# A batched matrix-product trace on one core: program layout, one-turn loops, and a third of the copies on VectorE

## The chip, the core and the metric

The kernel runs on one core of a Trainium2 chip. The core has TensorE (PE, a 128x128 matrix unit that writes to PSUM), VectorE (DVE), ScalarE (ACT), GpSimd (POOL, which here issues nearly all transfers) and SyncE (SP), each with its own stream of instructions; they meet through semaphores. Sixteen DMA engines move data between HBM and the on-chip SBUF; a transfer is spread over them in packets. The metric is the device time of one execution in microseconds (us).

## The reference

```python
B, N = 8, 2176
def reference(a, b):                       # a, b: (8, 2176, 2176) float32
    prod = np.matmul(a, b)
    traces = np.diagonal(prod, axis1=1, axis2=2).sum(axis=-1)
    return traces.astype(np.float32)       # (8,)
```

Only the trace is wanted, so no product is formed: for each batch the result is the sum over i and k of a[i, k] * b[k, i], that is, the elementwise product of a transposed with b, summed. All of a and b has to be read once, 303 MB in float32.

## The kernel before

The matrices are read with a cast to bf16 on the way (POOL issues, L182). 2176 is 17 blocks of 128. The rows of a matrix are taken in three groups of 6, 6 and 5 blocks (`six` for the two of 6, `five` for the last). For each of the eight batches:

- POOL loads the five-block part of a into `rows_b` (`five`) and the twelve-block part into `a_six`; then, as soon as the parts are free again, the five-block and the twelve-block part of b, both into `rows_b`. The waits ahead of these issues (on `made`, the count of finished transposes, and on `product`, the count of finished products) are what lets a buffer be written again.
- TensorE transposes a in 26 tiles (L226 to L246), 8 from `five` and 18 from `a_six`, into three PSUM slots (`SLOTS = 3`, tile n uses slot n % 3). Pairs of bf16 columns are moved as one float32 (L242), the odd ones as bf16 (L245). [...]
- ScalarE (L276) and VectorE (L302) copy the slots to `at`, the transposed a. VectorE takes the tiles with n % 4 == 3, ScalarE the other 20. The semaphores `free[k]` give the slot back to TensorE.
- VectorE multiplies `at` with b and sums (L291), once for the five-block part and once for the twelve-block part.

The last batch is closed differently: its b comes in ten pieces (`pieces`, semaphores `d_late`), from five blocks down to a part of one. VectorE takes the first 13 blocks' worth of columns of each row block, TensorE the other four by matrix products accumulated into `trace_ps`, whose diagonal holds what is wanted (L250 to L262: one product with zeros that opens the sum, a loop of 16 turns at L252 that waits on `landed`, and twelve products for the last row block). VectorE then takes the diagonal (L291 with `identity32`), TensorE adds over partitions (L332), VectorE reduces to eight numbers (L334) and SP stores them (L339).

In the order of the program, TensorE has the large loop first, then the products that close the last batch, then the total. The programs of ScalarE, VectorE and POOL are unrolled over the eight batches without a loop. POOL's ends with 20 increments of a semaphore `unread` that no one waits for, and a drain, after which the region ends for all engines.

Of the kernel before, what the change touches and what calls it, by code (L numbers as in the profile page):

```python
# [22 lines left out]
def kernel(  # L23
# [6 lines left out]
    nc = tc.nc  # L30
    P = 128
    BATCH, N, N2 = a.shape
# [84 lines left out]
    def rows_of(src, start, m, r0, r1):  # L117
        return src[start:start + P * m, :].rearrange("(p r) k -> p (r k)", r=m)[:, r0 * N:r1 * N]
# [25 lines left out]
    with tc.tile_critical(no_gpsimd_drain=True):  # L144
        def counted(name):
            return Counted(nc, name)

        unread = nc.alloc_semaphore("unread")
# [32 lines left out]
        def fetch(count, dst, src):  # L181
            count.by(gp.dma_start(out=dst, in_=src), 16)  # L182

        for n in range(BATCH):
            if n == 0:
                fetch(d_a5, flat(five[:, 1:, :]), rows_of(a[0], TWICE * P, FIVE, 1, FIVE))
                fetch(d_a6, a_six.rearrange(by_twos, g=2), six(a[0]))
                tc.wait_critical_data_deps()
                gp.wait_ge(zeros.sem, 2)
                for t in (identity32, identity16):  # L190
                    ready.by(gp.affine_select(
                        out=t, in_=t, compare_op=mybir.AluOpType.not_equal, fill=1.0, base=0,
                        pattern=[[-1, P]], channel_multiplier=1,
                    ))
            else:
                gp.wait_ge(product.sem, 2 * n - 1)
                fetch(d_a5, flat(five), rows_of(a[n], TWICE * P, FIVE, 0, FIVE))
                gp.wait_ge(made, EACH * n)
                if n < LAST:
                    fetch(d_a6, a_six.rearrange(by_twos, g=2), six(a[n]))  # L200
                else:
# [5 lines left out]
            gp.wait_ge(made, EACH * n + HEAD)  # L207
            if n < LAST:
                fetch(d_b5, flat(five), rows_of(b[n], TWICE * P, FIVE, 0, FIVE))
                if n:  # L210
                    gp.wait_ge(product.sem, 2 * n)
                fetch(d_b6, b_six.rearrange(by_twos, g=2), six(b[n]))
                continue
            for k, piece in enumerate(pieces):
                if k == 1:
                    gp.wait_ge(product.sem, 2 * n)
                fetch(d_late[k], piece.dst, piece.src)
        for _ in range(20):
            gp.sem_inc(unread)
        gp.drain()  # L220


        pe = nc.tensor
        pe.wait_ge(ready.sem, 3)
        alone = OrderedEngineSet([pe.engine])
        with nc.Fori(0, BATCH, engines=alone, hint_back_edge=True):  # L226
            for n, (moves, _, _) in enumerate(tiles):
                use, k = divmod(n, SLOTS)
                ps = slots[k]
                if n == 0:  # L230
                    pe.wait_ge(moved, 1)
                if use:
                    pe.wait_ge(free[k], 1 + use)
                else:
                    pe.wait_ge(free[k], 1 + uses[k]).then_inc(free[k], -uses[k])  # L235
                if n == HEAD:
                    pe.wait_ge(moved, 2)
                elif n == NECK:
                    pe.wait_ge(moved, 3).then_inc(moved, -3)
                for dtype, place, src in moves:  # L240
                    if dtype == f32:
                        last = pe.transpose(ps[:, place, :], src, identity32)  # L242
                    else:
                        ps16 = ps.bitcast(bf16).rearrange("q a b -> q (a b)")
                        last = pe.transpose(ps16[:, place * P:(place + 1) * P], src, identity16)  # L245
                last.then_inc(made, 1)  # L246

        pe.wait_ge(scalar_done.sem, BATCH)
        pe.wait_ge(vector_done.sem, BATCH)
        pe.matmul(trace_ps, diagonal, diagonal, start=True, stop=False)  # L250
        x, y = flat(at), flat(rows_b)
        with nc.Fori(SHARE, SHARE + END * N, N, engines=alone, hint_back_edge=True) as first:  # L252
            pe.wait_ge(landed, 1).then_inc(landed, -1)  # L253
            for c in range(ON_TENSOR):
                block = bass.ds(first + c * P, P)
                pe.matmul(trace_ps, x[:, block], y[:, block], start=False, stop=False)  # L256
        for k, piece in enumerate(pieces):
            if piece.v1 == NT:
                pe.wait_ge(d_late[k].sem, 16)
                for c in range(N - CLOSE * P if piece.hi == N else piece.lo, piece.hi, P):  # L260
                    block = slice(END * N + c, END * N + c + P)
                    ins = pe.matmul(  # L262
                        trace_ps, x[:, block], y[:, block],
                        start=False, stop=piece.lo == 0 and c + P == piece.hi,
                    )
        added.by(ins)


        act = nc.scalar
        for n in range(BATCH):  # L270
            for t in on_scalar:
                _, dst, view = tiles[t]
                if t == on_scalar[0] and n:
                    act.wait_ge(product.sem, 2 * n)
                act.wait_ge(made, EACH * n + t + 1)
                ins = act.copy(out=dst, in_=view(slots[t % SLOTS]))  # L276
                if t != on_scalar[-1]:
                    ins.then_inc(free[t % SLOTS], 1)
                else:
                    scalar_done.by(ins)  # L280


        dve = nc.vector
# [9 lines left out]
                op0=MUL, op1=ADD, accum_out=acc,  # L293
            )

        for n in range(BATCH):
            for t in on_vector:
                _, dst, view = tiles[t]
                if t == on_vector[0] and n:
                    dve.wait_ge(product.sem, 2 * n)  # L300
                dve.wait_ge(made, EACH * n + t + 1)
                ins = dve.tensor_copy(out=dst, in_=view(slots[t % SLOTS]))  # L302
                if t != on_vector[-1]:
                    ins.then_inc(free[t % SLOTS], 1)
                else:
                    vector_done.by(ins)
            dve.wait_ge(vector_done.sem, n + 1).then_inc(free[on_vector[-1] % SLOTS], 1)
            dve.wait_ge(scalar_done.sem, n + 1).then_inc(free[on_scalar[-1] % SLOTS], 1)  # L308
            if n == LAST:
                continue  # L310
            for k, (load, t, v0) in enumerate(((d_b5, five, 0), (d_b6, b_six, FIVE))):
                dve.wait_ge(load.sem, 16 * (n + 1))
                product.by(multiply_reduce(
                    flat(at[:, v0:v0 + t.shape[1], :]), flat(t), sums[:, TAKEN * n + k:TAKEN * n + k + 1],
                ))
        taken = TAKEN * LAST
        for k, piece in enumerate(pieces[:len(whole) + 1]):
            if piece is whole[-1]:
                dve.wait_ge(parts.sem, k)
                parts.by(dve.reduce_sum(  # L320
                    out=sums[:, taken:taken + 1], in_=late[:, 0:k], axis=mybir.AxisListType.X,
                ))
            close = piece.v1 == NT
            acc = sums[:, taken + 1 + close:taken + 2 + close] if close or piece is whole[-1] else late[:, k:k + 1]
            dve.wait_ge(d_late[k].sem, 16)
            x, y = (t[:, piece.v0:piece.v1, piece.lo:N - CLOSE * P if close else SHARE] for t in (at, rows_b))
            parts.by(multiply_reduce(x, y, acc))
        dve.wait_ge(added.sem, 1)
        parts.by(multiply_reduce(identity32, trace_ps, sums[:, taken + 3:], out=diagonal))

        pe.wait_ge(parts.sem, parts.count)
        summed.by(pe.matmul(total, ones, sums, start=True, stop=True))  # L332
        dve.wait_ge(summed.sem, 1)
        resulted.by(dve.reduce_sum(  # L334
            out=result[:1, :], in_=total.rearrange("o (b n) -> o b n", n=TAKEN),
            axis=mybir.AxisListType.X,
        ))
        sp.wait_ge(resulted.sem, 1)
        stored.by(sp.dma_start(  # L339
            out=out.rearrange("(a b) -> a b", a=1), in_=result[:1, :],  # L340
# [36 lines left out]
```

## Time and profile before

| | us |
|---|---|
| median of three runs (707.38 to 708.32) | 707.7 |
| profiled execution | 707.8 |
| its span, first to last instruction of the program | 705.8 |
| PE busy | 207.5 |
| DVE busy | 382.5 |
| ACT busy | 205.9 |
| POOL busy | 25.5 |

The span is shorter than the profiled execution's time by 2.0 us, which lie outside the program's own instructions. The busy times of the compute engines are shares of a span in which the transfers run all the time; the view by queue gives 152.12 MB written to SBUF (the half of what is read, by the cast) at a mean of 216 GB/s. In that view a queue is a row with its number of packets, the megabytes and the time of its packets as a share of 16 engines; the kind "instruction" is the transfer of program code to an engine's sequencer, "software_dynamic" are POOL's loads, "hardware_dynamic" the few that ACT and SP issue. Cut to a window, the same view counts the packets that start in it. In rows of the timeline the columns are start, duration, engine, line and operation, shapes, count, and in brackets the idle time before with what ended it; in the chain of waits they are start, duration and what the chain passed through.

### The profile page before, as it was taken

The numbers are of one execution on the slowest core, as the hardware profiler recorded it, in microseconds if no ns is written. First come the engines' busy times: TensorE is split into PE (matmuls) and PEld (weight loads), VectorE is DVE, ScalarE is ACT, GpSimd is POOL, SyncE is SP. The second block draws the span as 40 slices with busy tenths as digits, with TensorE's granted clock in tenths as the row PEclk, the third lists the DMA queues.
The fourth block names the chain that finished last, engine by engine and source line by source line (L and its number), as shares of the span: only waits on it lengthen the run. The fifth ranks groups of instructions, "written<-read, shape, count | busy, mean of one in ns | idle before, by whom it ended". The sixth has DMA issues, their size and how long they took to land.

```text
span 705.8 us, 3821 instructions
## 1 busy us (share of the span) xinstructions
PE 207.5 (29%) x1575; PEld 184.1 (26%) x1575; DVE 382.5 (54%) x101; ACT 205.9 (29%) x162; POOL 25.5 (4%) x47
## 2 busy tenths in 40 slices
PE   0335013440134401244013430124301353015633
PEld 0334012440124401243013430124301242014522
DVE  0105487153971539716396163961639617395388
ACT  1427003470034600336004450044500454005800
POOL 1000000000000000000000000000000000001100
PEclk9859555685556955569556785567855677555955
DMA  9999999999999999999999999999999999999998
GB/s 235 215 216 207 231 207 213 217 225 213 223 218 213 206 214 228 213 213 229 209 211 230 214 210 223 219 213 209 231 207 213 229 213 213 224 218 213 214 212 160
DMA packets 7846, 152.12 MB, mean 216 GB/s; under 512 B 674, under 2 KB 930, under 8 KB 1442
## 3 DMA queue, kind: packets, MB, share of 16 engines
q0 software_dynamic: 7696, 150.96, 99.8%
q10 hardware_dynamic: 144, 1.11, 0.5%
q8 instruction: 1, 0.02, 0.0%
q14 instruction: 3, 0.02, 0.0%
q1 hardware_dynamic: 2, 0.00, 0.0%
HBM read 303.04 MB, written 0.00 MB: 429 GB/s over the span
## 4 chain that ended last, share of the span: by engine, by line
DMA 34%; another core or an unknown queue 28%; DVE 15%; ACT 13%; PE 7%; issue 2%; POOL 1%; SPq 0%; DVEq 0%; POOLq 0%
DMA rows_b<-in_a_dram 21%; DVE at L291 15%; ACT at L276 13%; DMA rows_b<-in_b_dram 7%; DMA a_six<-in_a_dram 6%; PE aT L242 6%; PE aT L245 1%; POOL rows_b L182 1%; PE trace_ps L262 0%; DVE diagonal L291 0%; PE total L332 0%; DVE result L334 0%; DVE sums L291 0%; DVEq L308 0%
## 5 line engine op out<-in xcount | busy, mean ns | idle before, releaser
L276 ACT COPY at<-aT 128x1536 bf16<-128x1536 bf16 (+3 forms) x160 | 202.6, 1359 | 458.2 <-DVE sums L291 357.2
L291 DVE CUSTOM_DVE_ANT_0 at<-at,rows_b 128x10880 bf16<-128x10880 bf16 (+3 forms) x18 | 278.3, 15469 | 98.5 <-DMA rows_b<-in_b_dram 83.7
L302 DVE COPY at<-aT 128x1536 bf16<-128x1536 bf16 (+1 forms) x48 | 80.1, 1669 | 207.6 <-PE aT L242 156.1
L242 PE MATMUL aT<-identity,rows_b 128*128 128x128 f32 x240 | 55.4, 422 | 368.4 <-PEq L235 282.3
L242 PEld LDWEIGHTS aT<-identity,rows_b 128*128 128x128 f32 x240 | 47.1, 220 | 374.8 <-issue 283.2
L242 PE MATMUL aT<-identity,a_six 128*128 128x128 f32 x576 | 90.5, 320 | 93.7 <-SPq L173 80.5
L242 PEld LDWEIGHTS aT<-identity,a_six 128*128 128x128 f32 x576 | 83.3, 205 | 100.3 <-issue 89.4
L245 PE MATMUL aT<-identity,a_six 128*128 128x128 bf16 x480 | 34.3, 221 | 10.8 <-ACT at L276 9.5
L245 PEld LDWEIGHTS aT<-identity,a_six 128*128 128x128 bf16 x480 | 29.4, 119 | 15.2 <-ACT at L276 13.1
L291 DVE CUSTOM_DVE_ANT_1 at<-at,rows_b 128x3328 bf16<-128x3328 bf16 (+2 forms) x4 | 23.0, 5790 | 6.1 <-DMA rows_b<-in_b_dram 6.1
L182 POOL DMA_DIRECT2D rows_b<-in_b_dram x24 | 14.2, 613 | 330.0 <-PE aT L245 330.0
L245 PE MATMUL aT<-identity,rows_b 128*128 128x128 bf16 x200 | 17.7, 266 | 0.0
L245 PEld LDWEIGHTS aT<-identity,rows_b 128*128 128x128 bf16 x200 | 17.3, 135 | 0.5
L256 PE MATMUL trace_ps<-rows_b,at 128*128 x64 | 11.3, 285 | 20.6 <-PEq L253 20.6
L182 POOL DMA_DIRECT2D rows_b<-in_a_dram x8 | 4.6, 576 | 293.6 <-DVE sums L291 292.8
L256 PEld LDWEIGHTS trace_ps<-rows_b,at 128*128 x64 | 6.7, 104 | 25.2 <-issue 23.5
L182 POOL DMA_DIRECT2D a_six<-in_a_dram x9 | 6.1, 674 | 0.0
L284 DVE MEMSET ones<- 128x1 f32 x1 | 0.1, 59 | 8.1 <-ACT rows_b L142 8.1
L142 ACT CAST rows_b<-rows_b 128x2176 bf16<-128x2176 f32 x1 | 2.0, 2004 | 3.4 <-DMA rows_b<-in_a_dram 3.4
L262 PE MATMUL trace_ps<-rows_b,at 128*128 128x128 bf16 x12 | 1.5, 310 | 0.7 <-DMA rows_b<-in_b_dram 0.7
L142 ACT ACT_TABLE_LOAD x1 | 1.3, 1283 | 1.1 <-PEq L361 1.1
L291 DVE DVE_READ_ACCUMULATOR2_ANT sums<- 128x1 f32 x17 | 1.4, 83 | 0.0
(17 smaller groups left out, 4.3 us busy)
## 6 DMA issues: line engine op xcount, KB each, us to landing
a_six<-in_a_dram POOLq DMA_DIRECT2D x7, 6528.0 KB, 54.5
rows_b<-in_b_dram POOLq DMA_DIRECT2D x7, 6528.0 KB, 52.2
rows_b<-in_b_dram POOLq DMA_DIRECT2D x8, 2720.0 KB, 21.9
rows_b<-in_a_dram POOLq DMA_DIRECT2D x7, 2720.0 KB, 24.7
a_six<-in_a_dram POOLq DMA_DIRECT2D x2, 3264.0 KB, 47.0
rows_b<-in_a_dram POOLq DMA_DIRECT2D x1, 2176.0 KB, 14.8
rows_b<-in_b_dram POOLq DMA_DIRECT2D x1, 2176.0 KB, 31.0
rows_b<-in_b_dram POOLq DMA_DIRECT2D x2, 1088.0 KB, 38.0
```

What stands on the lines that cost most here:

```text
L142: nc.scalar.copy(out=five[:, 0, :], in_=words)
L182: count.by(gp.dma_start(out=dst, in_=src), 16)
L242: last = pe.transpose(ps[:, place, :], src, identity32)
L245: last = pe.transpose(ps16[:, place * P:(place + 1) * P], src, identity16)
L256: pe.matmul(trace_ps, x[:, block], y[:, block], start=False, stop=False)
L262: ins = pe.matmul(trace_ps, x[:, block], y[:, block], start=False, stop=piece.lo == 0 and c + P == piece.hi,)
L276: ins = act.copy(out=dst, in_=view(slots[t % SLOTS]))
L284: ready.by(dve.memset(ones, 1.0))
L291: return dve.tensor_tensor_reduce(out=x if out is None else out, in0=x, in1=y, scale=1.0, scalar=0.0, op0=MUL, op1=ADD, accum_out=acc,)
L302: ins = dve.tensor_copy(out=dst, in_=view(slots[t % SLOTS]))
```

## The change

Three things, in one diff.

1. The tiles with n % SLOTS == 2 go to VectorE (n = 2, 5, ..., 23, eight of 26) in place of n % 4 == 3 (six). As tile n uses slot n % 3, slot 2 is now emptied by VectorE alone and slots 0 and 1 by ScalarE alone.
2. The programs of POOL, ScalarE and VectorE stand in a loop each whose end is a register of value 1, which the program is told may be up to 8, so that a back edge with a hint is emitted though the loop turns once. POOL's and ScalarE's loops end with a wait for the last piece but one of b (`d_late[-2]`). ScalarE has a second loop, of two turns and without a hint, around the same wait. POOL's 20 increments are gone. The two loads and the identity of batch 0 stand ahead of POOL's loop.
3. TensorE's program has an outer loop of two turns. Turn 0 branches to the block "stream", which holds the large loop; turn 1 to the block "close", which stands ahead of it in the program and holds the closing products and the total. Both branch to "meet", the end. The loop over `landed` has lost its hint.

```diff
-    on_vector = [n for n in range(EACH) if n % 4 == 3]
-    on_scalar = [n for n in range(EACH) if n % 4 != 3]
+    on_vector = [n for n in range(EACH) if n % SLOTS == 2]
+    on_scalar = [n for n in range(EACH) if n % SLOTS != 2]
...
+        once = nc.alloc_register(gp.engine, "once")
+        gp.reg_mov(once, 1)
+        with nc.Fori(
+            0, gp.snap(once, min_val=1, max_val=BATCH), engines=OrderedEngineSet([gp.engine]),
+            hint_back_edge=True,
+        ):
+            for n in range(BATCH):
...
+            gp.wait_ge(d_late[-2].sem, 16)
-        for _ in range(20):
-            gp.sem_inc(unread)
         gp.drain()
...
+        with nc.Fori(0, 2, engines=alone) as turn:
+            fork = nc.cur_bb
+            pe.br_eq(turn, 1, on_true="close", on_false="stream")
+            with nc.body("close", valid_engines=alone):
+                pe.wait_ge(scalar_done.sem, BATCH)
+                pe.wait_ge(vector_done.sem, BATCH)
+                pe.matmul(trace_ps, diagonal, diagonal, start=True, stop=False)
...
+                with nc.Fori(SHARE, SHARE + END * N, N, engines=alone) as first:
...
+                added.by(ins)
+                pe.wait_ge(parts.sem, len(whole) + 3)
+                summed.by(pe.matmul(total, ones, sums, start=True, stop=True))
+                pe.br("meet")
+            with nc.body("stream", valid_engines=alone):
+                pe.wait_ge(ready.sem, 3)
+                with nc.Fori(0, BATCH, engines=alone, hint_back_edge=True):
...
+                pe.br("meet")
+            nc.switch_bb("meet", parent=fork)
...
+        once = nc.alloc_register(act.engine, "once")
+        act.reg_mov(once, 1)
+        with nc.Fori(
+            0, act.snap(once, min_val=1, max_val=BATCH), engines=OrderedEngineSet([act.engine]),
+            hint_back_edge=True,
+        ):
+            for n in range(BATCH):
...
+            act.wait_ge(d_late[-2].sem, 16)
+        with nc.Fori(0, 2, engines=OrderedEngineSet([act.engine])):
+            act.wait_ge(d_late[-2].sem, 16)
...
+        once = nc.alloc_register(dve.engine, "once")
+        dve.reg_mov(once, 1)
+        with nc.Fori(
+            0, dve.snap(once, min_val=1, max_val=BATCH), engines=OrderedEngineSet([dve.engine]),
+            hint_back_edge=True,
+        ):
+            for n in range(BATCH):
```

Inside the loops the instructions of POOL, ScalarE and VectorE and their waits are those of before, but for the tiles that changed hands. TensorE's instructions are the same.

More of the change, by code (lines that the diff above doesn't have):

```diff
@@ L182, in fetch @@
             count.by(gp.dma_start(out=dst, in_=src), 16)
[L184 to L199, printed above, removed]
+        fetch(d_a5, flat(five[:, 1:, :]), rows_of(a[0], TWICE * P, FIVE, 1, FIVE))
+        fetch(d_a6, a_six.rearrange(by_twos, g=2), six(a[0]))
+        tc.wait_critical_data_deps()
+        gp.wait_ge(zeros.sem, 2)
+        for t in (identity32, identity16):
+            ready.by(gp.affine_select(
+                out=t, in_=t, compare_op=mybir.AluOpType.not_equal, fill=1.0, base=0,
+                pattern=[[-1, P]], channel_multiplier=1,
+            ))
+        once = nc.alloc_register(gp.engine, "once")
[5 more added lines that the diff above has]
+            for n in range(BATCH):
+                if n:
+                    gp.wait_ge(product.sem, 2 * n - 1)
+                    fetch(d_a5, flat(five), rows_of(a[n], TWICE * P, FIVE, 0, FIVE))
+                    gp.wait_ge(made, EACH * n)
+                if 0 < n < LAST:
                     fetch(d_a6, a_six.rearrange(by_twos, g=2), six(a[n]))
-                else:
+                elif n == LAST:
                     for g, load in enumerate((d_a6, d_a12)):
@@ L206 @@
                         )
[L207 to L217, printed above, removed]
@@ L218 @@
-        for _ in range(20):
-            gp.sem_inc(unread)
+                gp.wait_ge(made, EACH * n + HEAD)
+                if n < LAST:
+                    fetch(d_b5, flat(five), rows_of(b[n], TWICE * P, FIVE, 0, FIVE))
+                    if n:
+                        gp.wait_ge(product.sem, 2 * n)
+                    fetch(d_b6, b_six.rearrange(by_twos, g=2), six(b[n]))
+                    continue
+                for k, piece in enumerate(pieces):
+                    if k == 1:
+                        gp.wait_ge(product.sem, 2 * n)
+                    fetch(d_late[k], piece.dst, piece.src)
@@ L220 @@
+            gp.wait_ge(d_late[-2].sem, 16)
         gp.drain()
         pe = nc.tensor
-        pe.wait_ge(ready.sem, 3)
         alone = OrderedEngineSet([pe.engine])
[L226 to L242, printed above, removed]
-                    else:
-                        ps16 = ps.bitcast(bf16).rearrange("q a b -> q (a b)")
-                        last = pe.transpose(ps16[:, place * P:(place + 1) * P], src, identity16)
-                last.then_inc(made, 1)
@@ L248 @@
[L248 to L266, printed above, removed]
@@ new lines @@
+        act = nc.scalar
+        once = nc.alloc_register(act.engine, "once")
[5 more added lines that the diff above has]
+            for n in range(BATCH):
+                for t in on_scalar:
+                    _, dst, view = tiles[t]
+                    if t == on_scalar[0] and n:
+                        act.wait_ge(product.sem, 2 * n)
+                    act.wait_ge(made, EACH * n + t + 1)
+                    ins = act.copy(out=dst, in_=view(slots[t % SLOTS]))
+                    if t != on_scalar[-1]:
+                        ins.then_inc(free[t % SLOTS], 1)
+                    else:
+                        scalar_done.by(ins)
+            act.wait_ge(d_late[-2].sem, 16)
@@ L294, in multiply_reduce @@
             )
[L296 to L337, printed above, removed]
+        once = nc.alloc_register(dve.engine, "once")
@@ new lines @@
+        dve.reg_mov(once, 1)
[4 more added lines that the diff above has]
+            for n in range(BATCH):
+                for t in on_vector:
+                    _, dst, view = tiles[t]
+                    if t == on_vector[0] and n:
+                        dve.wait_ge(product.sem, 2 * n)
+                    dve.wait_ge(made, EACH * n + t + 1)
+                    ins = dve.tensor_copy(out=dst, in_=view(slots[t % SLOTS]))
+                    if t != on_vector[-1]:
+                        ins.then_inc(free[t % SLOTS], 1)
+                    else:
+                        vector_done.by(ins)
+                dve.wait_ge(vector_done.sem, n + 1).then_inc(free[on_vector[-1] % SLOTS], 1)
+                dve.wait_ge(scalar_done.sem, n + 1).then_inc(free[on_scalar[-1] % SLOTS], 1)
+                if n == LAST:
+                    continue
+                for k, (load, t, v0) in enumerate(((d_b5, five, 0), (d_b6, b_six, FIVE))):
+                    dve.wait_ge(load.sem, 16 * (n + 1))
+                    product.by(multiply_reduce(
+                        flat(at[:, v0:v0 + t.shape[1], :]), flat(t), sums[:, TAKEN * n + k:TAKEN * n + k + 1],
+                    ))
+            taken = TAKEN * LAST
+            for k, piece in enumerate(pieces[:len(whole) + 1]):
+                if piece is whole[-1]:
+                    dve.wait_ge(parts.sem, k)
+                    parts.by(dve.reduce_sum(
+                        out=sums[:, taken:taken + 1], in_=late[:, 0:k], axis=mybir.AxisListType.X,
+                    ))
+                close = piece.v1 == NT
+                acc = sums[:, taken + 1 + close:taken + 2 + close] if close or piece is whole[-1] else late[:, k:k + 1]
+                dve.wait_ge(d_late[k].sem, 16)
+                x, y = (t[:, piece.v0:piece.v1, piece.lo:N - CLOSE * P if close else SHARE] for t in (at, rows_b))
+                parts.by(multiply_reduce(x, y, acc))
+            dve.wait_ge(added.sem, 1)
+            parts.by(multiply_reduce(identity32, trace_ps, sums[:, taken + 3:], out=diagonal))
+            dve.wait_ge(summed.sem, 1)
+            resulted.by(dve.reduce_sum(
+                out=result[:1, :], in_=total.rearrange("o (b n) -> o b n", n=TAKEN),
+                axis=mybir.AxisListType.X,
+            ))
```

47 lines of the change are left out of this document (34 added, 13 removed).

## The prediction

> **What bounds the kernel now.** I read the page's queue lines first, then the transfers by window, the chain of waits at the end, and last the copies by shape.
>
> ```profile
> span 705.8 us, 3821 instructions
> ...
> DMA  9999999999999999999999999999999999999998
> ...
> q8 instruction: 1, 0.02, 0.0%
> q14 instruction: 3, 0.02, 0.0%
> ```
> The digits of the 16 DMA engines are 9 in all but the last fortieth. The same view cut to 4.9 to 702.1 us says how full that is:
>
> ```profile
> DMA packets 7719, 151.04 MB, mean 217 GB/s; under 512 B 670, under 2 KB 926, under 8 KB 1438
> ...
> q0 software_dynamic: 7694, 150.95, 101.1%
> ```
> So 697.2 of the 705.8 us are the transfer of a and b with no engine resting (packets overlap a little, so the share passes 100%). The compute engines matter in two places only: where they could let the queue run dry, and behind the last byte. Whether it can run dry is read from issue to landing:
>
> ```profile
> a_six<-in_a_dram POOLq DMA_DIRECT2D x7, 6528.0 KB, 54.5
> rows_b<-in_b_dram POOLq DMA_DIRECT2D x7, 6528.0 KB, 52.2
> rows_b<-in_b_dram POOLq DMA_DIRECT2D x8, 2720.0 KB, 21.9
> rows_b<-in_a_dram POOLq DMA_DIRECT2D x7, 2720.0 KB, 24.7
> ```
> At 217 GB/s a load of 2720 KB needs 12.8 us and one of 6528 KB 30.8 us. The rest of the time to landing is queue still ahead of it: 9.1 us for the five-row load of b, 11.9 for that of a, 21.4 and 23.7 for the twelve-row loads. Every stage may be 9 us later before an engine idles.
>
> Behind the last byte stands this chain of waits, and one DMA issue from the timeline:
>
> ```profile
> 653.66 47.79 DMA rows_b<-in_b_dram
> ...
> 701.50 1.48 PE trace_ps L262 x12
> ...
> 703.00 0.29 DVE diagonal L291
> ...
> 703.35 0.28 PE total L332 x2
> ...
> 703.65 0.18 DVE result L334
> ```
> ```profile
> 703.86 0.32 SPq L339 DMA_DIRECT2D out_dram<-result  x1
> ```
> From the last byte (702.1) to the result is 1.7 us, and 2.0 more to the end of the span. The time of the profiled execution, 707.8, has 2.0 us outside the span. It stands 0.1 over the median 707.7 of the three runs.
>
> **The change part by part.** *Every third copy on VectorE.* The copies by shape:
>
> ```profile
> L276 ACT COPY at<-aT 128x1536 bf16<-128x1536 bf16 x96 | 130.8, 1461 | 86.8 <-PE aT L242 86.7
> L276 ACT COPY at<-aT 128x1280 bf16<-128x1280 bf16 x40 | 46.7, 1231 | 369.7 <-DVE sums L291 357.2 <-PE aT L242 12.6
> ```
> ```profile
> L302 DVE COPY at<-aT 128x1536 bf16<-128x1536 bf16 x32 | 56.2, 1758 | 154.8 <-PE aT L242 124.6 <-PE aT L245 30.2
> L302 DVE COPY at<-aT 128x1280 bf16<-128x1280 bf16 x16 | 23.9, 1492 | 52.8 <-PE aT L242 31.5 <-PE aT L245 21.2
> ```
> VectorE had tiles 3, 7, ..., 23, six of 26; it gets 2, 5, ..., 23, eight: two of 1280 columns and six of 1536. Per batch VectorE gains two copies of 1536, 2 x 1.758 = 3.5 us, and ScalarE loses 2 x 1.461 = 2.9 us; over eight batches +28 and -23. Before, ScalarE's three of four tiles took 3 x 1.461 = 4.4 us per four, 1.10 a tile; after, its two of three take 2.9 per three, 0.97, with VectorE's 1.76 beside them. ScalarE still paces, and the 18 tiles of the twelve-row part end up to 18 x 0.13 = 2.3 us sooner. If the slot that VectorE alone serves (number 2) paced instead, at most 8 x 1.76 = 14.1 us a batch, it would still be under ScalarE's ten copies of 1536 alone, 14.6. The worst end I take from the rows is the added 3.5 us a batch falling on the chain. Both ends lie inside the 9.1 us of queue, so this part counts 0; without that cover it would be -2.3 to +3.5 us a batch.
>
> *Loops of one turn around the programs of POOL, ScalarE and VectorE.* Each gains a few register moves, one jump, one hint and one compare; POOL and ScalarE also wait for the last piece but one of b before they leave, ScalarE then twice more in a loop of two turns. POOL's 39 remaining issues keep their order and waits, the 20 increments of an unread semaphore go. Behind the new waits only the program's end is queued, and that end stands behind the result of 703.83 anyway, so the waits (met by 702.1 to 702.5) count 0. What the hint can change is where instructions are fetched from memory, and the page has those as transfers of their own. Cut to 195.9 to 196.9 us, around the first of the three of q14 (the other two have the same share in such a window):
>
> ```profile
> q14 instruction: 1, 0.01, 2.0%
> ```
> 2.0% of 16 engines for 1 us is 0.32 us of one engine. That one engine then ends its share of the data 0.32 us after the others, and a load has landed only when the slowest engine has. The trace bears it out on the last packets of 8704 bytes (a row of 4352 numbers of two bytes), one an engine: 13 start between 690.28 and 690.70, and three stragglers (five packets, two of them small) between 690.70 and 690.95:
>
> ```profile
> DMA packets 13, 0.11 MB, mean 269 GB/s; under 512 B 0, under 2 KB 0, under 8 KB 0
> ```
> ```profile
> DMA packets 5, 0.03 MB, mean 122 GB/s; under 512 B 1, under 2 KB 1, under 8 KB 2
> ```
> Three fetches, three stragglers. If the hints hold the three fetches back until the loops are left, the last byte moves from the stragglers' latest to the others': between 0 and 0.32 us earlier. The edges of the two windows are 0.25 apart, near the upper bound, so I take -0.3. That there are three fetches, and that three engines get a loop, is my reason to ascribe them to these engines; the views don't name the owner.
>
> *TensorE's last products ahead of its large loop.* The same instructions run in the same order of time, plus a jump to the large loop and, after its eight turns, a jump back to the products and one onward to the end. The jump back falls here:
>
> ```profile
> 668.60 0.23 PE L250 MATMUL trace_ps<-diagonal 128*128 128x128 bf16 x1 [1.52 <-ACT at L276]
> 671.31 8.82 DVE L291 CUSTOM_DVE_ANT_1 at<-at,rows_b 128x8320 bf16<-128x8320 bf16 x1 [4.69 <-DMA rows_b<-in_b_dram]
> ...
> 681.87 0.72 PE L256 MATMUL trace_ps<-rows_b,at 128*128 x4 [4.44 <-PEq L253]
> ```
> The first diagonal product starts at 668.60 and the first piece of b is only there at 671.31: 2.7 us free, and 4.4 more idle before the second piece's products. So the jump counts 0. The inner loop loses its hint: one sequencer instruction a turn, between waits for data, 0. The onward jump stands behind the product of 703.35 and lies beside the store of the result (703.86 and on); 0, or what the second rival makes of it. TensorE's own fetch is the one of q8, in 701.7 to 702.8:
>
> ```profile
> q8 instruction: 1, 0.02, 5.6%
> ```
> 5.6% of 16 engines for 1.1 us is 0.99 us of one engine, after that engine's data, so it delays nothing now. That it is TensorE's I conclude from its size, unlike the three others, and its place behind TensorE's last loop. Moving it costs between nothing and 0.99 us on one engine.
>
> *Sum.* By the profiled execution 707.8 - 0.3 + 0 = 707.5 us, by the median of the runs 707.4.
>
> **The rivals.** *The hints hold nothing back.* The fetches stay where they are; 707.7. For it: a hint towards a loop's head need not stop what comes next in order. Against it: TensorE's large loop has such a hint, and its q8 shows not one fetch in 0 to 701.7 us.
>
> *The end of the program is fetched late (the slower side).* An engine leaves its loop, or TensorE jumps to the end, and the code there isn't loaded. Place: behind 703.63, where the data no longer hides anything. Price from the fetch of q8, which is over by 702.8, and TensorE's last turn ahead of it, which ends at 700.8, so some 2.0 us:
>
> ```profile
> 700.04 0.74 PE L256 MATMUL trace_ps<-rows_b,at 128*128 x4 [1.92 <-PEq L253]
> ```
>  It decides when the code is missing after the total product; the store of the result then hides from nothing to all of it. At full price 707.4 + 2.0 = 709.4. For it: the jump onward is a new far one, in an idle stretch of 2.2 us. Against it: POOL and ScalarE leave at 702.1 to 702.5, in time for a fetch of 2.0 us to be done by the span's last microsecond.
>
> *TensorE fetches during the data.* With the products ahead, the fetch of q8 may come when the large loop is left, near 667. Its engine then ends 0.99 us later, less its lead over the last of the 13, which start within 0.42 us: +0.57 to +0.99, about 708.2.
>
> [...]
>
> *The 2.0 us outside the span shrink.* If most of them are such fetches behind the last instruction and these now come at 702, up to 1.5 could go: 705.9. No row of the trace shows that stretch.
>
> **How the numbers follow.** Forecast (707.4) 0.46; hints without effect (707.7) 0.17; TensorE's fetch in the data (708.2) 0.10; late end (709.4) 0.15; loop not loaded (715 to 723) 0.05; outside the span (705.9) 0.07. A change of 0.2%, 1.4 us, is about what a measurement of this kernel can tell from none: 706.3 and 709.1 are the bounds. Faster 0.07; same 0.46 + 0.17 + 0.10 = 0.73; slower 0.20. The range reaches from 706.9 (the forecast with the 0.5 by which single runs differ) to 709.6 (the late end at full price), which leaves out the two far cases, 0.12, and a little at the edges. Within the same sign the likeliest alone has 706.9 to 708.0.
>
> **What would show it.** Right: no q14 transfer between 5 and 701 us; the last packets of 8704 bytes within 0.45 us of each other; ScalarE's copies down to 144 and VectorE's up to 64; the queue's share unchanged at 101%. The chain behind the last byte keeps its 1.7 us. Wrong: q8 or q14 transfers in the middle, DMA digits under 9, an idle stretch between the total product (703.4) and the end longer than 2.3 us, or a time over 709.1 or under 706.3.

## The result and the profile after

| | before | after |
|---|---|---|
| median, 20 runs each | 707.53 (707.14 to 708.32) | 709.09 (708.84 to 709.69) |
| profiled execution | 707.8 | 708.94 |
| its span | 705.8 | 707.2 |

The changed kernel takes 1.0021 times as long, interval 1.0015 to 1.0028: slower by 1.6 us, a small loss, but one that the interval sets apart from none. The forecast was 707.4; the rival of the late end had 709.4.

The page of the changed kernel, its span, the DMA digits and the rows of the instruction queues:

```profile
span 707.2 us, 3818 instructions
...
DMA  9999999999999999999999999999999999999997
...
q8 instruction: 1, 0.02, 0.0%
q14 instruction: 1, 0.01, 0.0%
```
The transfers by queue, cut to 4.9 to 701.6 us, which is up to the last byte:

```profile
DMA packets 7717, 151.01 MB, mean 217 GB/s; under 512 B 672, under 2 KB 928, under 8 KB 1440
...
q0 software_dynamic: 7696, 150.96, 101.1%
q10 hardware_dynamic: 21, 0.04, 0.0%
```
There is no instruction row left in this window: the three fetches of q14 in the data are gone, and the queue is as full as before. The last packets of 8704 bytes, cut to 689.98 to 690.43 us and then to 690.43 to 690.70:

```profile
DMA packets 16, 0.14 MB, mean 309 GB/s; under 512 B 0, under 2 KB 0, under 8 KB 0
```
```profile
DMA packets 4, 0.01 MB, mean 32 GB/s; under 512 B 2, under 2 KB 2, under 8 KB 4
```
All sixteen start within 0.45 us, and behind them come four small packets and no straggler. The chain of waits at the end, and the store from the timeline:

```profile
652.98 47.99 DMA rows_b<-in_b_dram
...
701.01 1.48 PE trace_ps L246 x12
...
702.51 0.29 DVE diagonal L312
...
702.87 0.28 PE total L252 x2
...
703.17 0.18 DVE result L359
```
```profile
703.38 0.31 SPq L364 DMA_DIRECT2D out_dram<-result  x1
```
The result is there at 703.35, 0.48 us earlier than before (703.83). Yet the span ends at 707.2: from the result to the end it was 2.0 us and is now 3.8. What SyncE, which closes the program, waits for says where they are; of these two rows (line, what it waited for, total, times, longest) the same view of before has only the first, at its own lines:

```profile
SPq L364 <- DVE result L359: 4.1, 1, 4.1
SPq L144 <- PEq L144: 2.3, 1, 2.3
```
L144 is the line at which the engines meet when the program ends. SyncE stands there 2.3 us for TensorE's sequencer. The transfers cut to 703 to 708 us have TensorE's fetch:

```profile
q8 instruction: 1, 0.02, 1.1%
q14 instruction: 1, 0.01, 0.5%
```
Before, the q8 fetch lay in 701.7 to 702.8, beside the closing products; now it stands behind the total product. By the records of single instructions, TensorE leaves its outer loop at 703.43, the fetch runs from 703.93 to 704.85, and TensorE's next instruction is at 706.20.

A second engine is late, hidden behind the first. POOL now starts its drain only at 701.81 and needs 3.42 us for it (the three durations, in ns, are the least, the median and the longest of the one drain):

```profile
L223 POOLq DRAIN  x1: 3417/3417/3417, 701.8 to 701.8; - x1
```
POOL reaches the meeting at 705.81. Before, its drain was over at 704.14 and it was at the meeting at 704.26, with the others. That SyncE would have to wait for POOL shows only once TensorE is out of the way, in the first experiment. The copies, by shape:

```profile
L294 ACT COPY at<-aT 128x1536 bf16<-128x1536 bf16 x80 | 110.3, 1446 | 93.2 <-PE aT L272 93.0
L329 DVE COPY at<-aT 128x1536 bf16<-128x1536 bf16 x48 | 84.4, 1758 | 142.7 <-PE aT L272 126.9 <-PE aT L275 15.7
```
Sixteen copies of 1536 columns went from ScalarE to VectorE, at the same 1.45 and 1.76 us each.

### The profile page after: what moved, and what is told of

Same layout as the page of the kernel before. It is cut to its first block, busy times and chain, and to the rows that moved or that the text cites. A ratio compares the mean times of both kernels' runs of the same rounds, so it can differ in the third digit from the quotient of the medians.

```text
span 707.2 us, 3818 instructions
## 1 busy us (share of the span) xinstructions
PE 204.4 (29%) x1575; PEld 182.1 (26%) x1575; DVE 410.6 (58%) x117; ACT 185.5 (26%) x146; POOL 25.6 (4%) x47
## 4 chain that ended last, share of the span: by engine, by line
DMA 35%; another core or an unknown queue 28%; DVE 14%; ACT 11%; PE 8%; issue 3%; POOL 1%; SPq 0%; DVEq 0%; POOLq 0%
DMA rows_b<-in_a_dram 22%; DVE at L312 14%; ACT at L294 11%; PE aT L272 7%; DMA rows_b<-in_b_dram 7%; DMA a_six<-in_a_dram 6%; PE aT L275 1%; POOL rows_b L181 1%; DVE at L329 0%; PE trace_ps L246 0%; DVE diagonal L312 0%; PE total L252 0%; DVE sums L312 0%; DVE result L359 0%
## 5 line engine op out<-in xcount | busy, mean ns | idle before, releaser
L294 ACT COPY at<-aT 128x1536 bf16<-128x1536 bf16 (+1 forms) x144 | 182.2, 1333 | 477.3 <-DVE sums L312 364.3
L329 DVE COPY at<-aT 128x1536 bf16<-128x1536 bf16 (+1 forms) x64 | 108.2, 1691 | 178.1 <-PE aT L272 162.2
L275 PEld LDWEIGHTS aT<-identity,rows_b 128*128 128x128 bf16 x200 | 15.8, 129 | 0.8 <-ACT at L294 0.2
```

## The experiments

The kernel before was timed beside each group: 707.59 for the first four runs, 707.52 for the next four, 707.39 for the third, 707.43 for the last. Ratios are to these, with their 95% interval.

**Which part costs the time.** `e1_pe_back` is the changed kernel with TensorE's program as before, `e2_pool_back` with POOL's as before, `e3_pe_pool_back` with both, and `e4_copies_only` the kernel before with the copies moved. The edits of e1 and e2 are told in short, the others are lines of the edits.

```diff
 # e1: from after            # e2: from after
-with nc.Fori(0, 2, ...)    -with nc.Fori(0, snap(once)): all issues
-"close", "stream", "meet"  -    gp.wait_ge(d_late[-2].sem, 16)
+large loop, then products  +all issues unrolled, 20 increments
+and total, inner hint back  gp.drain()
 # e4: from before
-on_vector = [n for n in range(EACH) if n % 4 == 3]
+on_vector = [n for n in range(EACH) if n % SLOTS == 2]
```


> The changed kernel with TensorE's program as before (large loop, closing products, total, in that order); the loops of POOL, ScalarE and VectorE and the new copies stay. Theory (two engines are late at the end, one beside the other: TensorE waits for a fetch of its code, and POOL, whose drain stands behind the new wait, ends that drain only at 705.2): TensorE's q8 transfer is back near 701, the SP wait on TensorE's end (2.3 us) is gone, but POOL's lateness remains and the time falls only a little, 708.5 to 709.0. Rival A (TensorE alone is the cause): 707.0 to 707.3. Rival B (POOL alone): 709.1, nothing changes. Rival C (the copies on VectorE cost it): 709.1.

> The changed kernel with POOL's program as before (unrolled, 20 increments, then the drain; no wait for the last piece but one); the rest stays changed. Theory: POOL is on time again (its drain ends near 703.7), one q14 transfer is back in the middle; TensorE is still 2.3 us late, so 709.0 to 709.4. Rival A (TensorE alone): the same, 709.0 to 709.4. Rival B (POOL alone): 707.0 to 707.5. Rival C (copies): 709.1.

> Both taken back: what stays of the change are the copies and the loops of ScalarE and VectorE. Theory: nobody is late at the end, two of three q14 transfers are gone from the middle, 707.0 to 707.5, at or a little under before (707.5). Rival A: the same, and equal to the run with TensorE's program alone taken back. Rival B: the same, and equal to the run with POOL's program alone taken back. Rival C (copies or the two loops left cost it): 709 still.

> The kernel before with every third copy on VectorE and nothing else. Theory: hidden behind the transfers, 707.3 to 707.7, three q14 transfers in the middle and the drain as before. Rival C: up to 709, with the chain of the batches (copies, then products) reaching the transfers, so that the queue's share falls under 100% somewhere.

Measured: e1 709.16 (1.0023, 1.0012 to 1.0033), e2 709.38 (1.0024, 1.0015 to 1.0033), e3 707.25 (1.0000, 0.9991 to 1.0009), e4 707.42 (1.0002, 0.9993 to 1.0011). In the medians undoing either part gives nothing back, undoing both gives all of it. SyncE's waits at the end of e1 and of e2 say why:

```profile
SPq L144 <- POOLq L144: 1.8, 1, 1.8
```
```profile
SPq L144 <- PEq L144: 2.8, 1, 2.8
```
With TensorE's program as before the end waits for POOL, with POOL's it waits for TensorE: two late ends of nearly one size, side by side, of which the view of after could name only the later. e1 was expected at 708.5 to 709.0 and lies above. Its runs fall in two groups, four at 708.5 (spans 706.8) and four from 709.8 on (707.7 to 707.9); the profiled one is of the second. In that one q8 is fetched inside the data, at 675 us. The same is seen in the profiled execution of e3 (708.62, the slowest of its eleven), cut to 668 to 677 us:

```profile
q8 instruction: 1, 0.02, 0.6%
```
0.6% of 16 engines for 9 us is 0.9 us of one engine, and the last byte then comes at 702.6 in e1 and e3, against 701.6 and 701.8 in after and e4, where the fetch starts at 703.9 and at 701.6. Over all the profiled executions, the seven with this fetch between 670 and 676 us have the last byte at 702.45 to 702.76, the eleven others at 701.58 to 702.12. Spans of other executions fall into two groups too (of the kernel before, beside e1 to e4: 705.4 to 705.7 and 706.0 to 706.3). I put that down to where this one fetch falls, but only one execution of each kernel was profiled; the medians are over both kinds.

**POOL: the drain behind the wait.** `e8_late_drain_alone` puts the late wait into the kernel before; `e5_drain_first` takes it from ahead of the drain of the changed kernel.

```diff
 # e8: from before
+gp.wait_ge(d_late[-2].sem, 16)
 gp.drain()
 # e5: from after, still inside the loop
-gp.wait_ge(d_late[-2].sem, 16)
+gp.drain()
+gp.wait_ge(d_late[-2].sem, 16)
-gp.drain()        # behind the loop
```


> The kernel before with one edit: POOL waits for the last piece but one before its drain. Theory: the drain starts near 702.2 and takes 3.4 us, POOL meets the others near 706.2 in place of 704.3, time 708.7 to 709.3 against 707.6. Rival (the drain ends 2 us behind the last data whenever it starts, and costs only where a loop is left ahead of it): 707.5 to 707.8.

> The changed kernel with POOL's drain moved ahead of its wait for the last piece but one (both inside the loop); TensorE as changed. Theory (POOL's drain takes 3.4 us when it starts behind the last data and is over in time when it starts at 655; TensorE's late fetch is a second, independent lateness): POOL meets the others near 703.8, TensorE still keeps SP waiting for some 2.3 us, time unchanged at 709.0 to 709.4. Rival (the drain alone, TensorE's fetch is hidden without it): 707.0 to 707.5.

e8: 708.26 (1.0011, 1.0002 to 1.0020). The wait alone costs 0.7 us (0.1 to 1.4 by the interval), less than the 708.7 to 709.3 expected. Its profiled execution shows the row that the kernel before lacks:

```profile
SPq L144 <- POOLq L144: 1.0, 1, 1.0
```
The drain takes 3.42 us again when it starts with the last of the data. Where it is started early, at 652 to 656 us, it ends 2.0 to 2.1 us behind the last byte (704.14 before, 704.52 in e5, last bytes 702.12 and 702.51). Most of what e8 lacks to the 1.8 us of e1 is a step of 0.6 us between the end of the drain, or of the loop, and the meeting. Every run with POOL's loop has it (0.57 to 0.59 us), e8 has 0.04; I had reckoned with it in e8. The loop isn't shown to be its cause: all these runs lack the 20 increments too, and e12 below, which has no loop on POOL and no increments, has 0.81 us there (703.57 to 704.38, with SyncE's call to the meeting at 703.69).

e5, at 709.27 (1.0025, 1.0015 to 1.0036), is as slow as the changed kernel, as expected. That TensorE is what still comes late there is concluded, not seen: the profiled execution is the one short one of eight (708.11), with q8 fetched at 670.2, TensorE in time and SyncE waiting 0.3 us for POOL. The seven others, at 709.1 to 709.6, have spans like that of e7 below (707.3 to 707.8), and e7, which has the drain first too, was profiled with TensorE late.

**TensorE: why its end is late.** A first idea was that only TensorE's last few instructions need the fetch. `e6_close3` makes TensorE's closing part three products shorter (in the last row block it has nine of the 17 blocks in place of twelve; in the others it keeps four), `e7_drain_first_close3` does so with POOL's drain first.

```diff
-ON_TENSOR, TAKEN, CLOSE = 4, 4, 6
+ON_TENSOR, TAKEN, CLOSE = 4, 4, 3
```


> The changed kernel with three blocks fewer of the last row block on TensorE (VectorE takes 1024 columns there in place of 640): TensorE's program is six instructions shorter, so that its last instructions move out of the block that is fetched at the end. Theory: the q8 transfer is not needed before the meeting of the engines, SP no longer waits for TensorE; POOL's drain stays late, so the span ends near 706.8, time 708.5 to 708.9. Rival (not the place in the block, but the jump out of the closing block costs the 2.8 us): SP waits as before, 709.1. In both VectorE's longer last product adds nothing, since TensorE's diagonal is ready later.

> Both edits together: drain ahead of the wait, and TensorE's program six instructions shorter. Theory: no one is late, result near 703.4, span 705.2 to 705.5, time 707.0 to 707.3, at or under the kernel before (707.6). Rival (the fetch only moves behind the span, and the time outside the span grows by it): span 705.3, but time 708.5 to 709.5.

e6 709.22 (1.0024, 1.0014 to 1.0033), e7 709.28 (1.0024, 1.0014 to 1.0034), SyncE's wait for TensorE 2.8 and 2.6 us: no effect, against both theories. The next four took the parts of TensorE's change one at a time: `e9_pe_only` is the kernel before with TensorE's new layout alone, `e10_no_inner_hint` is e3 without the hint of the loop over `landed`, `e11_no_outer_loop` is the changed kernel with plain jumps in place of the outer loop, and `e12_no_padding` is e3 without the 20 increments. For e9 the edit is TensorE's part of the change.

```diff
 # e10: from e3
-with nc.Fori(SHARE, SHARE + END * N, N, engines=alone, hint_back_edge=True) as first:
+with nc.Fori(SHARE, SHARE + END * N, N, engines=alone) as first:
 # e11: from after
-with nc.Fori(0, 2, engines=alone) as turn:
-    pe.br_eq(turn, 1, on_true="close", on_false="stream")
+pe.br("stream")       # stream ends with pe.br("close"), close with pe.br("meet")
 # e12: from e3
-for _ in range(20):
-    gp.sem_inc(unread)
```


> The kernel before with TensorE's new layout alone (closing products and total ahead of the large loop, outer loop of two turns). Theory (TensorE's code for the end is fetched only when the outer loop is left behind the total, and costs SP 2.3 us and more): q8 transfer near 704, SP waits for TensorE, 709.0 to 709.8 in most executions. Rival (it was POOL's drain and the layout is harmless): 707.3 to 707.8.

> The run with TensorE's and POOL's programs taken back, and the hint taken off TensorE's loop of 16 turns (L252 of the kernel before). There the q8 transfer fell at 675 in the profiled execution and the last byte came near 702.6 in place of 701.6. Theory (a q8 transfer during the data holds one DMA engine back by its 0.9 us, and the hint in that loop is what calls for it there): transfer behind the data, last byte near 701.6, span near 705.2, 707.0 to 707.2 in all executions. Rival (the hint keeps it away, and without it the fetch always falls in the data): 707.9 to 708.6 in all.

> The changed kernel with TensorE's outer loop taken out: a plain jump to the large loop, from its end a plain jump back to the closing products, from their end a plain jump to the end. Order in memory and order in time as changed. Theory (leaving the outer loop at 703.4 is what starts the fetch): without that loop the fetch is not started there; either it comes when the large loop is left (one engine 0.9 us late, TensorE on time, POOL's drain decides, 708.4 to 708.7) or on the jump to the end. Rival (the place of the end's code decides, whatever branch leads there): q8 near 703.7 and 708.8 to 709.4, as changed.

> The run with TensorE's and POOL's programs taken back, without POOL's 20 increments of the unread semaphore. Theory (they move the fetch of POOL's end into the data, where it costs one engine 0.32 us but is loaded in time): without them no q14 transfer between 5 and 701 us, last byte up to 0.3 earlier; if POOL then fetches at the end it meets the others some 2 us late, 708.5 to 709; if its end needs no further code, 706.9 to 707.2. Rival (the increments do nothing): q14 at 657 as before and 707.1 to 707.4.

e9 707.55 (1.0003, 0.9994 to 1.0012): the layout alone costs nothing, against the theory. Its fetch, however, is as late as in the changed kernel; cut to 703.2 to 706 us:

```profile
q8 instruction: 1, 0.02, 2.3%
```
It starts at 704.19, and TensorE is at the meeting at 704.05, before it: here the fetch isn't needed for the end, in the changed kernel it is. By the records of single instructions the fetch starts 0.48 us after TensorE leaves its outer loop in e9, and 0.50 to 0.52 us after it in the six profiled executions in which SyncE waits for TensorE (after, e2, e6, e7, and e13 and e14 below). In these six TensorE's next instruction comes 1.35 to 1.46 us behind the end of the fetch, whenever that is (704.85 to 705.45); this is what ties the wait to the fetch.

e10 708.03 (1.0008, 0.9999 to 1.0017): without the inner hint the profiled execution has the fetch in the data, at 675.6, and all eleven spans are 706.0 to 706.5, where e3 and e12 have most at 705.3 to 705.6. By these spans the hint of this loop is what usually keeps TensorE's fetch out of the data in the layout of before; the other ten executions of e10 were not profiled. e11 709.64 (1.0031, 1.0018 to 1.0043) has the fetch in the data too, at 675.4; TensorE is then in time, and SyncE waits 1.7 us for POOL. It lies above the 708.4 to 708.7 expected for this, because POOL's drain starts behind a last byte that is itself 0.9 us late (702.49, after 701.61). e12 707.23 (0.9998, 0.9989 to 1.0008): the increments cost nothing that can be told. But without them, and without a loop on POOL, the fetch near 657 us is gone; one of the same size stands behind the data instead, at 705.2. So the increments decide where that fetch falls, as the theory of e12 had it.

Open by then was why the same program of TensorE is in time in e9 and late in e2. Three kernels add one thing each to e9: ScalarE's loops (`e13_pe_and_act_loops`), VectorE's loop (`e14_pe_and_dve_loop`), or eight more instructions on TensorE ahead of its large loop (`e15_pe_longer`, 3823 instructions in all where e9 has 3815). The fourth, `e16_pe_back_drain_first`, is e5 with TensorE's program as before.

```diff
 # e15: from e9 (sixteen waits)
-pe.wait_ge(ready.sem, 3)
+for _ in range(16):
+    pe.wait_ge(ready.sem, 3)
```


> The kernel before with TensorE's new layout (on time by itself, 707.55) and ScalarE's loops alone; copies, POOL and VectorE stay. Theory (each loop that another engine gets puts one more step into TensorE's way to the end, and the end falls out of what TensorE has loaded): SyncE waits for TensorE 2.3 to 2.8 us at line 144 and the time is 708.9 to 709.6. Rival (it takes VectorE's loop, or the copies): no such wait, 707.2 to 708.0.

> The kernel before with TensorE's new layout and VectorE's loop alone; copies, POOL and ScalarE stay. Theory (any further loop makes TensorE's end late): SyncE waits for TensorE 2.3 to 2.8 us at line 144, 708.9 to 709.6. Rival (ScalarE's loops, or the copies, do it): no such wait, 707.2 to 708.0.

> The kernel before with TensorE's new layout and eight more instructions that wait for what is long there, ahead of TensorE's large loop; no loop on any other engine. Theory (it is the place of TensorE's end that counts: a few instructions further back it lies outside what is loaded): the fetch of 16384 bytes is waited for, 708.9 to 709.6. Rival (loops of other engines are needed): on time, 707.2 to 708.0.

> The changed kernel with TensorE's program as before and POOL's drain ahead of its late wait: the loops of POOL, ScalarE and VectorE and the copies stay. Theory (the two late ends, POOL's and TensorE's, are all that the change loses): 707.0 to 707.6, POOL behind its loop still 0.6 us but its drain done by 704.6. Rival (a hinted loop around POOL's program costs at the end however its drain stands): 708.0 or more, SyncE waiting for POOL over 1 us.

e14 709.49 (1.0028, 1.0017 to 1.0038). The wait for TensorE, absent in e9, is there:

```profile
SPq L144 <- PEq L144: 2.7, 1, 2.7
```
e13 has it too, at 2.6 us, and a span of 707.8 like e14's (707.7), but takes 712.08 (1.0057, 1.0044 to 1.0071), which is above both theories; its profiled execution took 711.78, so 4.0 us lie outside the span. The transfers of e13 behind the span, 707.8 to 713 us, have two fetches of 8192 bytes that e14 and the kernel before do not have there:

```profile
q14 instruction: 2, 0.02, 1.1%
```
e15, without any loop on another engine, 709.33 (1.0023, 1.0014 to 1.0032): nine of eleven runs at 709.0 to 709.8, as the theory of place has it. The other two, at 707.8 and 707.9, include the profiled one, and there the fetch was early, cut to 668 to 674 us:

```profile
q8 instruction: 1, 0.02, 1.0%
```
At 670.2 it costs the data 0.5 us (last byte 702.45, e9 701.93) and saves the end; that the nine others had it late is concluded from their spans of 707.3 to 708.0, which were not profiled. So a loop on one other engine (profiled) or, by these spans, eight instructions more make TensorE wait for its end to be fetched. Why a loop on another engine does, although TensorE's own program then is written the same, stays open: the views don't show where the program lies in memory.

e16 707.30 (1.0002, 0.9993 to 1.0011), as expected. It keeps the loops of POOL, ScalarE and VectorE and the copies, and SyncE's waits at the end shrink to

```profile
SPq L144 <- POOLq L144: 0.3, 1, 0.3
SPq L144 <- PEq L144: 0.2, 1, 0.2
```
With both late ends gone nothing of the loss is left. Nor is a gain: none of e3, e12 and e16 can be told from the kernel before.

## Why the prediction was wrong

*The copies, 0: right.* e4 shows nothing, and the queue is as full as before.

*The hinted loops, -0.3: the size fits, the cause holds for two loops of three, and the times can't tell it.* The three fetches left the data and the result came 0.48 us earlier in the profiled executions. But the final reduction of e4, which still has all three fetches, starts at 703.37 (703.65 before), so 0.3 us of that lies between executions of kernels with the same fetches. Over all the profiled executions without a q8 fetch in the data, the last byte comes at 701.58 to 701.78 in the five without a q14 fetch there (after, e6, e7, e12, e16) and at 701.81 to 702.12 in the five with two or three (before, e4, e9, e13, e14): 0.26 us between the means, one execution of each kernel (e2, with one, has 701.59). The three stragglers were a weaker sign: the last sixteen packets of 8704 bytes start within 0.43 to 0.57 us of each other in the first five and within 0.64 to 0.74 in the others. In medians e3, e12 and e16 are 0.13 to 0.34 us under the kernel before, all inside their intervals. In the trace a hint is a record of its own on the engine of the loop: L226 has eight before, one a turn (9.3 to 589.3 us), and after has one each on POOL (L194, 8.9), ScalarE (L284, 8.3) and VectorE (L319, 8.5). That a load has landed only with its slowest part shows in the records too: before, the last piece of b has its sixteen landing marks from 701.80 to 702.42, and TensorE's wait for it passes at 702.46. Whose the fetches are can now be read from single parts: e13, with ScalarE's loops, lacks the one near 196 us, e14, with VectorE's, that near 388. So these two programs' loops keep a fetch each out of the data, as the step had it. The one near 657 is gone where POOL has its loop (e16), but also in e12, where POOL has none and only the increments are missing. The change took these away too, so nothing shows that POOL's loop holds anything back.

*"Behind the new waits only the program's end is queued [...] so the waits count 0": wrong.* What is queued behind POOL's wait is its drain, and the step took it for free because the result comes later than the wait is met. The wait is met near 701.7, but the drain then takes 3.42 us and ends 1.9 us behind the result; started early it ends 0.3 us behind it. That costs 0.7 us alone (e8) and, with the 0.6 us behind the drain, a wait of 1.8 us (e1). No row of before has the 3.42 us, since the drain started there at 655.77; but it ended there at 704.14, 0.1 us ahead of the meeting, which left no room for starting it later.

*"The onward jump [...] 0, or what the second rival makes of it": the 0 was wrong, and the rival was right about TensorE.* TensorE's end is fetched behind the total product, and SyncE waits 2.3 us (2.6 to 2.8 in e2, e6, e7, e13, e14). The price of 2.0 us from the old q8 row was near. The jump itself finds its target: two instructions of the outer loop, at 703.25 and 703.35, run right behind it. The fetch stands behind the step out of that loop, which the prediction did not list; the rival, which spoke of leaving a loop or of a jump, covers it. The forecast gave the rival 0.15, and the argument against it, that POOL and ScalarE leave early enough, spoke of two engines that have nothing to do with TensorE's jump. After, e13 and e14 have a wait of 2.3 to 2.7 us behind the branch that ends the outer loop. That TensorE's end would need no wait was the author's estimate, and it does not hold: every profiled execution has a q8 fetch between 670 and 705 us, and in after TensorE's end waits for it.

*The sum.* Forecast 707.4; the end is later than its terms by the growth from result to end of span, 3.8 - 2.0 = 1.8 us. 707.4 + 1.8 = 709.2, measured 709.09. The 1.8 us are not the two late ends added but the later of them: with TensorE's program as before, POOL alone still keeps the time at 708.5 and more (e1). That the time lies near the rival's 709.4 is therefore in part luck, since the rival had only one of the two ends. The signs of being right came true as well: no q14 transfer in the data, the packets within 0.45 us, the counts of the copies, the queue at 101%, 1.7 us from the last byte to the result. None of them looked past the result. Of the signs of being wrong, "an idle stretch between the total product and the end longer than 2.3 us" is the one that came true: 703.15 to SyncE's release at 706.2 is 3.1 us.

*TensorE fetches during the data, 708.2:* did not happen in the profiled execution of the changed kernel, but does in that of e10 (708.03), near the price given, and in those of e1, e3, e5, e8, e11 and e15. *Loop not loaded, 715 to 723:* no run shows this term; in before and after the eight turns of the large loop, the last branch of which is at 666.7 and 665.5 us, have no q8 fetch, and in every profiled execution the only one within the span lies between 670 and 705 us. *The 2.0 us outside the span:* 1.7 to 1.8 in the 20 runs of after, and 4.0 to 4.3 in e13, the other way.

## What to carry to other kernels

When the data sets the time, look at what each engine still has to do behind its last wait, its drain (3.42 us here) and the step out of its last loop (a wait of 2.3 to 2.8 us here, where the end was fetched behind it) included: a wait of no cost ahead of a drain of 3.42 us is not free. Two engines late by nearly the same amount (waits of 1.8 us in e1 and 2.8 in e2) hide each other, so undoing one part of a change shows little; undo both, and each alone. What the data may win (0.26 us between the means) is lost at once where one fetch moves from beside the closing work to behind it (2.3 us in after). Look too at which execution was profiled: in e5 and e15 it was not one of the usual kind.

## What the runs showed of the hardware

- One fetch of 16384 bytes takes 0.92 to 1.37 us on one DMA engine. In the data it moves the last byte by 0.5 to 1.0 us (e15 against e9, e3 against e12), behind TensorE's arrival at the meeting it costs nothing that can be told (e9), and in front of TensorE's last instructions SyncE waits 2.3 to 2.8 us. By the spans, where it falls differs between executions of the same kernel (e1, e3, e15).
- POOL's drain takes 3.42 us when it starts within 0.2 us of the last byte, in after, e1, e6, e8 and e11 alike. Started at 652 to 656 us it ends 2.0 to 2.1 us behind the last byte.
- The time outside the span, 1.7 to 2.4 us elsewhere (2.7 in one run of e1), was 4.0 to 4.3 in all five runs of e13; the profiled one has two fetches of 8192 bytes behind the last instruction. The profiled ones of e1 and e3 have one of 16384 bytes there, with 2.0 and 2.4 us outside. Why e13 and not e14 was not tried.
